# Low weight parts of 24 input-projection blocks by adding transfers, and one buffer set for high and low parts

## The chip, the cores and the metric

The kernel runs on one core of a Trainium2 chip. The metric is the device time of one launch in microseconds (us), a median over runs. Beside it stands one execution recorded by the hardware profiler; its durations are what the text argues from.

## The reference

One layer of a bidirectional hybrid encoder on 512 tokens of 1024 channels, all in float32:

```python
h = rmsnorm(x, mix_norm[l])
p = h @ w_in[l]                                   # 1024 x 9248
rx, ry, qkv, z, ba, gates = jnp.split(p, SPLIT_IDX, axis=-1)
y_rnn = rglru_branch(rx, ry, ...) @ w_rnn_proj[l]
y_dn = deltanet_branch(qkv, z, ba, ...) @ w_dn_proj[l]
g_rnn, g_dn = jnp.split(jax.nn.sigmoid(gates), 2, axis=-1)
x = x + (g_rnn * y_rnn + g_dn * y_dn) @ w_out[l]
h = rmsnorm(x, ffn_norm[l])
gt, up = jnp.split(h @ w_gate_up[l], 2, axis=-1)
x = x + (jax.nn.silu(gt) * up) @ w_down[l]
...
return rmsnorm(x, final_norm)
```

The part that matters here is `p = h @ w_in`: 72 blocks of 128 output columns (and 32 single columns for `ba`).

## The kernel before, in words

**Products in three parts.** A float32 product on TensorE is made of float32r products. A weight block is split into a high part (the weight rounded to float32r) and a low part (the weight less its high part); the activations likewise (`hh`, `hl`). A block's product is high × `hh` + high × `hl` + low × `hh`. `mm3` issues, for a block of 1024 × 128 weights and 512 tokens, 16 matmuls with the high part (`hh` and `hl` in turn, one pair for each of eight slices of 128 rows) and then 8 with the low part: 24 matmuls of 128 × 512. The low part is so wanted 16 matmuls later than the high part.

**How a block's weights come in.** `stage`, through `weights`, plans four steps: SyncE's queue (SP) loads 512 KB into a raw buffer (`wraw`, four of them), ScalarE (ACT) copies it into the high part (`whi`, a CAST from float32 to float32r), VectorE (DVE) subtracts the high part from the raw weights into the low part (`wlo`), and TensorE (PE) uses both. There are two `whi` and two `wlo` buffers of 128 × 1024. The first three blocks use buffers of their own (`weights_k`). The blocks of the other weight matrices use the same three tags.

**The order of the work.** The program isn't written in the order in which it runs. Every operation is recorded (`Rec`), with an estimate of its cost and a planned time `plan.t`; a block's load is planned 40 us ahead of its use, its split 12 (`AHEAD`). `Plan.order` then sets one static sequence for each engine by a list scheduler that starts from the table `TIMES`, a starting time for each of some 200 stages. Everything is emitted from that order, so all instructions carry line 384 in the profile and are told apart by tile names. Each engine works strictly in its sequence; waits between engines are semaphores. A buffer that is used again is waited for: the copy into `whi` waits for the last matmul that reads the block before in that buffer.

**Where the 72 blocks lie.** `in_proj` is called for the blocks of the two recurrent branches, of the queries, keys and values of four head groups (`dn_front`), of `dn_z` and of the two gates (`rnn_gate`, `dn_gate`). It appends to `first_tiles`, which so counts the blocks planned. Between them PE works on the recurrences, the small chunk matrices of the delta rule and the output projection. The feed-forward part (`gate_up`, `down_first`, `down_second`) follows from some 640 us on.

GpSimd (POOL) has little to do: constants and nine small loads in the first 14 us, later 48 small multiplications and 32 selects on the delta rule's matrices.

Of the kernel before, what the change touches and what calls it, by code (L numbers as in the profile page):

```python
# [8 lines left out]
F32R = mybir.dt.float32r  # L9
AF = mybir.ActivationFunctionType  # L10
ALU = mybir.AluOpType
# [3 lines left out]
P = 128  # L15
# [3 lines left out]
KD = D // P  # L19
# [13 lines left out]
RELEASE = 200  # L33
LOOK = 40
TIMES = [
# [14 lines left out]
]  # L50
ENGINES = ("PE", "DVE", "ACT", "POOL", "SP")
N2, N4, NW = 15, 24, 4
AHEAD = 12.0
# [271 lines left out]
class Rec:  # L325
# [5 lines left out]
    def __getattr__(self, op):  # L331
        real = getattr(self.real, op)

        def call(*a, **kw):
            args = list(a) + list(kw.values())
            aps = [x for x in args if hasattr(x, "ap") and hasattr(x, "tensor")]
            out = kw.get("out", a[0] if a else None)
            outs = [out] + ([kw["accum_out"]] if kw.get("accum_out") is not None else [])
            ins = [x for x in aps if not any(x is o for o in outs)]
            big = [x for x in ins if elems(x) > 1 or x.space == PSUM]  # L340
            n = max([elems(out)] + [elems(x) for x in ins])
            psum = any(x.space == PSUM for x in aps)
            ptr = sum(1 for x in ins if elems(x) == 1) if n > 1 else 0
            table, tail = None, 0.0
            e = self.eng
            if op == "dma_start":
                tail = max(out.nbytes() / 360.0, 1)
                cost = 450 if e == "SP" else 1000 if e == "POOL" else 60
            elif e == "PE":
                rhs = a[2] if op == "matmul" else a[1]  # L350
                n = elems(out)
                four_ = rhs.dtype == F32
                cols = elems(a[1]) if op == "matmul" else P
                if op == "transpose":
                    cost = 110
                elif four_:
                    cost = 22 if cols == 32 else 76 if cols == 64 else n * 4 / 2.4 + 10
                else:
                    cost = max(n / 2.4, 107) + 13.3
            elif e == "ACT":  # L360
                cost = (51 if psum else 93) + 0.834 * n + 93 * (ptr if n > 1 else len(ins) - 1) + (93 if len(outs) > 1 else 0)
                if op == "activation":
                    cost = max(cost, 200)
                dims = list(out.ap)
                if op == "copy" and len(dims) > 2 and dims[-1][1] <= 64:
                    cost += 100
                if op == "activation":
                    table = Plan.TABLES.get(a[2])
            elif e == "DVE":
                if op == "reciprocal":  # L370
                    cost = 69 + 6.25 * n
                elif op == "tensor_tensor":
                    cost = 69 + 1.042 * n
                elif op == "tensor_tensor_scan":
                    cost = 69 + 2.08 * n
                elif op == "scalar_tensor_tensor":
                    cost = 130 + 1.042 * n + (70 if len(outs) > 1 else 0)
                elif op == "transpose":
                    cost = 68 + (2.0 if n > 512 else 1.1) * n
                else:  # L380
                    cost = 68 + (1.042 if psum else 0.521) * n + 61 * ptr
            else:
                cost = {"memset": 35 + 0.834 * n, "affine_select": 140 + 0.886 * n}.get(op, 240 + 1.2 * n)
            self.plan.add(e, lambda: real(*a, **kw), outs, ins, cost, tail, table)  # L384

        return call
# [3 lines left out]
def trunk(ctx: ExitStack, tc: tile.TileContext, x, mix_norm, w_in, rg_conv_w, rg_conv_b, rg_wa, rg_ba, rg_wx, rg_bx,  # L390
# [3 lines left out]
    plan = Plan(nc)  # L394
    V, A, G, T = Rec(plan, "DVE", nc.vector), Rec(plan, "ACT", nc.scalar), Rec(plan, "POOL", nc.gpsimd), Rec(plan, "PE", nc.tensor)
    Q = Rec(plan, "SP", nc.sync)
# [3 lines left out]
    wp = ctx.enter_context(tc.tile_pool(name="wp", bufs=2))  # L400
# [14 lines left out]
    def new(pool, shape, tag, bufs, dt=F32):  # L415
        return plan.tile(pool, shape, dt, tag, bufs, nm(tag))
# [13 lines left out]
    def four(dt=F32, shape=(P, 2, 512)):  # L430
        return new(t4, shape, "t4", N4, dt)
# [17 lines left out]
    def f(ap):  # L449
        return ap.bitcast(F32)  # L450
# [143 lines left out]
    first_tiles = []  # L594

    def stage(src, shape, view=lambda t: t, admit=()):

        now = plan.t
        raw = new(wp, shape, "wraw", NW)
        hi = new(wp, shape, "whi", 2, F32R)  # L600
        lo = new(wp, shape, "wlo", 2, F32R)
        plan.t = now - 40
        for dst, s_ in src(raw):
            Q.dma_start(dst, s_)
        plan.t = now - AHEAD
        plan.admit = admit
        A.copy(view(hi), view(raw))
        plan.admit = ()
        V.tensor_tensor(view(lo), view(raw), f(view(hi)), ALU.subtract)
        plan.t = now  # L610
        return hi, lo

    def weights(src, kk, m=P, admit=()):
        return stage(lambda raw: [(raw[:, :kk, :m], src)], (P, 8, P), lambda t: t[:, :kk, :m], admit)

    def parts_of(src, hi, lo, ahead):
        now = plan.t
# [23 lines left out]

    def in_proj(col, po=None, admit=()):
        spend(5.2)
        hi, lo = (weights_k if len(first_tiles) < 3 else weights)(win[:, :, col:col + P], KD, P, admit)
        po = mmb() if po is None else po
        mm3(po, hi, lo, lambda k: hh[:, k, :], lambda k: hl[:, k, :], KD, 2 if len(first_tiles) < 3 else 1)
        first_tiles.append(col)
        return po
# [16 lines left out]
    G.dma_start(dtb, dn_dt_bias[0].rearrange("d h -> (d h)").partition_broadcast(P))  # L665
    G.dma_start(alog, dn_a_log[0].rearrange("d h -> (d h)").partition_broadcast(P))
    braw = new(wp, (P, 8, P), "wraw", NW)
    bhl = new(wp, (P, 8, P), "whi", 2, F32R)
    Q.dma_start(braw[:, :, 0:32], win[:, :, C_BA:C_BA + 32])
    A.copy(bhl[:, :, 0:32], braw[:, :, 0:32])  # L670
    V.tensor_tensor(bhl[:, :, 32:64], braw[:, :, 0:32], f(bhl[:, :, 0:32]), ALU.subtract)
# [618 lines left out]
        T.matmul(po, xl[:, cs_], wh, start=False, stop=stop, skip_group_check=add)  # L1290

    def halves(src, own=False):
        hi, lo = (new(wp, (P, 2, 512), t, 2, F32R) if own else four(F32R) for t in ("whi", "wlo"))
        parts_of(src, hi, lo, 0)
        return [(hi[:, i, :], lo[:, i, :]) for i in range(2)]

# [150 lines left out]
    def gate_up(n):  # L1447
        spend(10.2)
        now = plan.t
# [7 lines left out]
        for t, x_, y_ in ((t1, b11, b12), (t2_, t1, b22), (t3, b12, b22), (t4_, t2_, b21)):  # L1457
            V.tensor_tensor(t, x_, y_, ALU.add)
        plan.t = now
        gh_, gl_ = new(wp, (P, 8, P), "whi", 2, F32R), new(wp, (P, 8, P), "wlo", 2, F32R)  # L1460
        parts_of(rg, gh_, gl_, AHEAD)
        w7 = {"1": (gh_[:, 0:4, :], gl_[:, 0:4, :]), "2": (gh_[:, 4:8, :], gl_[:, 4:8, :])}
        ah, al = new(wp, (P, 8, P), "whi", 2, F32R), new(wp, (P, 8, P), "wlo", 2, F32R)
        bh, bl = four(F32R, (P, 8, P)), four(F32R, (P, 8, P))
        for i, (name, src, hi, lo) in enumerate((("6", t2_, ah, al), ("7", t3, ah, al), ("5", t1, bh, bl), ("4", t4_, bh, bl))):
            j = 4 * (i % 2)
# [68 lines left out]
    def down_first(j):  # L1535
# [1 line left out]
        spend(5.5)  # L1537
        now = plan.t
        r1, r2 = new(wp, (P, 2, 512), "wraw", NW), new(wp, (P, 2, 512), "wraw", NW)
        hi, lo = new(wp, (P, 2, 512), "whi", 2, F32R), new(wp, (P, 2, 512), "wlo", 2, F32R)  # L1540
        t2_ = keep2[j // 8][:, j % 8, :]
        plan.t = now - 40
        Q.dma_start(r2, sums[j])
# [177 lines left out]
```

## Time and profile before

| | |
|---|---|
| median of 3 runs | 1054.76 us (1054.02 to 1055.81) |
| profiled execution | 1052.97 us, of which the span 1051.1 |
| granted TensorE clock | 0.999 |
| busy: PE, DVE, ACT, POOL | 1037.1, 891.1, 689.5, 54.4 us |
| moved | 134.35 MB, mean 128 GB/s |

The profiled execution is one launch; its span runs from the first to the last instruction, and 1.9 us of its time lie around the span. "PEld" is TensorE's weight load, which runs beside its matmuls. In a group's row stand: line, engine, operation, result and operands, shape and count, then busy time in us and the mean of one in ns, then idle time ahead of the group and what ended it. In a row of the timeline stand start and duration in us, and in brackets the idle time ahead of it and its releaser.

### The profile page before, as it was taken

What the parts mean: (1) busy time and instruction counts of PE and PEld (TensorE: products, weight loads), DVE (VectorE), ACT (ScalarE), POOL (GpSimd) and SP (SyncE); (2) the same over time, 40 slices, a digit from 0 to 9 for tenths busy, and PEclk for the clock granted to TensorE, in tenths of its full rate; (3) what the DMA queues carried; (4) which work ended last, traced back from release to release, by engine and by line L of the source; (5) the groups of instructions that cost most, each with busy time, mean ns of one, the idle gap of its engine ahead of it and who ended that gap; (6) DMA issues with size and microseconds to landing.
All of it is one profiled execution on the core that took longest, in us unless ns stands there. A gap on an engine that the chain in (4) does not pass through costs nothing.

```text
span 1051.1 us, 17768 instructions
## 1 busy us (share of the span) xinstructions
PE 1037.1 (99%) x6707; PEld 905.0 (86%) x6707; DVE 891.1 (85%) x1650; ACT 689.5 (66%) x1265; POOL 54.4 (5%) x109
## 2 busy tenths in 40 slices
PE   8999999999999999999999999999999999999997
PEld 7888788888888978888788798889999999998886
DVE  7769989658894898589489748999999999889997
ACT  7799898696638868564765434578554554456564
POOL 2000000202000222010020000000000000000000
PEclk9999999999999999999999999999999999999999
DMA  9422223225342246523213414597456443326632
GB/s 281 121 70 80 81 61 110 71 66 145 101 117 60 74 113 193 182 79 105 57 41 91 141 32 150 188 332 253 139 157 198 147 143 109 122 85 216 215 107 80
DMA packets 177396, 134.35 MB, mean 128 GB/s; under 512 B 6400, under 2 KB 161168, under 8 KB 177312
## 3 DMA queue, kind: packets, MB, share of 16 engines
q1 hardware_dynamic: 175840, 129.95, 40.7%
q10 hardware_dynamic: 1184, 3.15, 0.8%
q8 instruction: 52, 0.85, 0.3%
q14 instruction: 32, 0.26, 0.1%
q0 software_dynamic: 288, 0.13, 0.1%
HBM read 121.12 MB, written 12.09 MB: 127 GB/s over the span
## 4 chain that ended last, share of the span: by engine, by line
PE 91%; DVE 5%; ACT 2%; issue 1%; DMA 1%; ACTq 0%; SPq 0%; DVEq 0%
PE mm L384 53%; PE ax L384 23%; PE st L384 15%; DVE t L384 3%; DVE na L384 1%; ACT t L384 1%; DVE wlo L384 1%; DMA wraw<-in_w_in_dram 1%; ACT hh L384 0%; ACTq L384 0%; ACT L384 0%; ACT whi L384 0%; SPq L384 0%; DVE so L384 0%; DVE hl L384 0%
## 5 line engine op out<-in xcount | busy, mean ns | idle before, releaser
L384 DVE TENSOR_TENSOR t<-t,t 128x512 fp32r<-128x512 f32 (+26 forms) x501 | 249.4, 512 | 24.1 <-ACT t L384 15.8
L384 PE MATMUL mm<-hh,whi 128*128 128x512 f32 (+2 forms) x648 | 228.1, 362 | 0.1
L384 PE MATMUL mm<-hl,whi 128*128 128x512 f32 (+2 forms) x648 | 228.0, 361 | 0.0
L384 ACT CAST whi<-wraw 128x1024 fp32r<-128x1024 f32 (+3 forms) x139 | 130.3, 939 | 122.6 <-PE mm L384 74.9
L384 DVE TENSOR_TENSOR wlo<-wraw,whi 128x1024 fp32r<-128x1024 f32 (+2 forms) x138 | 150.6, 1092 | 40.8 <-ACT whi L384 19.6
L384 PE MATMUL ax<-t,t 128*128 128x512 f32 (+3 forms) x1134 | 156.9, 291 | 1.6 <-issue 1.6
L384 PE MATMUL mm<-hh,wlo 128*128 128x512 f32 (+1 forms) x632 | 147.3, 364 | 0.1
L384 PEld LDWEIGHTS ax<-t,t 128*128 128x128 f32 (+1 forms) x1134 | 123.1, 161 | 21.5 <-issue 3.5
L384 PEld LDWEIGHTS mm<-hh,whi 128*128 128x128 f32 (+1 forms) x648 | 121.6, 188 | 17.5 <-DVE whi L384 0.3
L384 PEld LDWEIGHTS mm<-hl,whi 128*128 128x128 f32 (+1 forms) x648 | 121.6, 188 | 17.1
L384 PEld LDWEIGHTS mm<-hh,wlo 128*128 128x128 f32 x632 | 108.6, 189 | 17.7 <-DVE wlo L384 0.5
L384 ACT CAST t<-t 128x512 fp32r<-128x512 f32 (+2 forms) x148 | 94.9, 654 | 43.7 <-DVE t L384 33.9
L384 DVE SCALAR_TENSOR_TENSOR t<-mm,par,t 128x511 f32<-128x511 f32 (+1 forms) x108 | 80.2, 743 | 18.7 <-ACT t L384 17.7
L384 ACT ACT_TABLE_LOAD x66 | 84.7, 1283 | 6.5 <-DVE so L384 2.0
L384 PE MATMUL mm<-t,whi 128*128 128x512 f32 x320 | 83.2, 397 | 1.2 <-DVE t L384 1.2
L384 PE MATMUL mm<-t,t 128*128 128x256 f32 (+1 forms) x420 | 80.3, 330 | 0.0
L384 PEld LDWEIGHTS mm<-t,whi 128*128 128x128 f32 x320 | 59.0, 188 | 13.1 <-issue 1.6
L384 PEld LDWEIGHTS mm<-t,t 128*128 128x128 f32 x420 | 63.8, 190 | 6.6
L384 ACT ACTIVATE t<-t 128x128 f32<-128x128 f32 (+4 forms) x86 | 47.4, 561 | 31.4 <-DVE t L384 29.9
L384 ACT CAST t<-wraw 128x1024 fp32r<-128x1024 f32 (+1 forms) x55 | 49.2, 896 | 23.3 <-DMA wraw<-in_w_gate_up_dram 14.5
L384 DVE TENSOR_TENSOR t<-wraw,t 128x1024 fp32r<-128x1024 f32 (+1 forms) x55 | 56.6, 1032 | 1.1 <-ACT t L384 0.7
L384 PE MATMUL mm<-t,wlo 128*128 128x512 f32 x160 | 42.9, 394 | 0.0
(208 smaller groups left out, 1685.5 us busy)
## 6 DMA issues: line engine op xcount, KB each, us to landing
wraw<-in_w_in_dram SPq DMA_DIRECT2D x72, 512.0 KB, 3.7
wraw<-in_w_gate_up_dram SPq DMA_DIRECT2D x44, 512.0 KB, 4.4
wraw<-in_w_rnn_proj_dram SPq DMA_DIRECT2D x16, 384.0 KB, 3.5
wraw<-in_w_out_dram SPq DMA_DIRECT2D x12, 512.0 KB, 3.5
t<-in_w_down_dram SPq DMA_DIRECT2D x11, 512.0 KB, 7.1
sums<-t SPq DMA_DIRECT2D x11, 512.0 KB, 5.1
wraw<-sums SPq DMA_DIRECT2D x11, 512.0 KB, 3.4
wraw<-in_w_down_dram SPq DMA_DIRECT2D x22, 256.0 KB, 3.3
```

Source lines behind the costliest of these rows:

```text
L384: self.plan.add(e, lambda: real(*a, **kw), outs, ins, cost, tail, table)
```

## The change

- `weights_d` is new. It loads the raw block as before, lets ACT copy the high part, lets ACT write the negated high part into the low buffer, and then has POOL issue a transfer (`accum_op=ALU.add`) that adds the raw block, 512 KB from one on-chip buffer to another, to what stands in the low buffer: raw − high. DVE has no part in it. ACT's two steps are planned 14 us ahead of use in place of 12.
- `in_proj` uses it from the 49th block planned on, for 24 blocks of 72.
- The tags `whi` and `wlo`, two buffers each, become one tag `wx` with four, for all that used them.
- The planner takes twice the moving time for an adding transfer.
- `TIMES` holds new numbers, so the order of the whole program is another.

```diff
 TIMES = [
-    -176998, -159417, -176656, -106634, -96501, -159195, -96162, -70221, 191167, -94063, -87550, -69365, -34065,
+    -162283, -159297, -163526, -108037, -92752, -158970, -94346, -59098, 168648, -70151, -72611, -51972, -22916,
...
             if op == "dma_start":
-                tail = max(out.nbytes() / 360.0, 1)
+                tail = max(out.nbytes() / 360.0, 1) * (2 if "accum_op" in kw else 1)
...
         raw = new(wp, shape, "wraw", NW)
-        hi = new(wp, shape, "whi", 2, F32R)
-        lo = new(wp, shape, "wlo", 2, F32R)
+        hi = new(wp, shape, "wx", 4, F32R)
+        lo = new(wp, shape, "wx", 4, F32R)
...
+    def weights_d(src, admit):
+
+        now = plan.t
+        raw, hi, lo = new(wp, (P, 8, P), "wraw", NW), new(wp, (P, 8, P), "wx", 4, F32R), new(wp, (P, 8, P), "wx", 4, F32R)
+        plan.t = now - 40
+        Q.dma_start(raw, src)
+        plan.t = now - AHEAD - 2
+        plan.admit = admit
+        A.copy(hi, raw)
+        plan.admit = ()
+        A.activation(lo, f(hi), AF.Copy, scale=-1.0)
+        G.dma_start(lo, raw, accum_op=ALU.add)
+        plan.t = now
+        return hi, lo
...
         spend(5.2)
-        hi, lo = (weights_k if len(first_tiles) < 3 else weights)(win[:, :, col:col + P], KD, P, admit)
+        if len(first_tiles) < 48:
+            hi, lo = (weights_k if len(first_tiles) < 3 else weights)(win[:, :, col:col + P], KD, P, admit)
+        else:
+            hi, lo = weights_d(win[:, :, col:col + P], admit)
...
-    bhl = new(wp, (P, 8, P), "whi", 2, F32R)
+    bhl = new(wp, (P, 8, P), "wx", 4, F32R)
...
-        gh_, gl_ = new(wp, (P, 8, P), "whi", 2, F32R), new(wp, (P, 8, P), "wlo", 2, F32R)
+        gh_, gl_ = new(wp, (P, 8, P), "wx", 4, F32R), new(wp, (P, 8, P), "wx", 4, F32R)
```

(The other buffers of `halves`, `gate_up` and `down_first` change their tags in the same way.)

What the new order does at one place, around a gate block of `dn_gate` or `rnn_gate` (`mm932_1012` is its result). Before, DVE had the subtraction between small vectors of the delta rule (`na`, `dns`, `t` are its working tiles):

```order
L384 TENSOR_TENSOR wlo853_933<-wraw851_931,whi852_932 128x1024
L384 TENSOR_TENSOR t21013_1093<-mm1009_1089,t497_177 128x512
L384 TENSOR_SCALAR n2842_922<-dssq836_916 128x8
L384 RECIPROCAL n2842_922<-n2842_922 128x8
L384 TENSOR_TENSOR dns865_945<-beta68_148,n2842_922 128x16
L384 TENSOR_TENSOR dnse866_946<-dns865_945,ge83_163 128x16
L384 TENSOR_TENSOR wlo931_1011<-wraw929_1009,whi930_1010 128x1024
L384 SCALAR_TENSOR_TENSOR na867_947<-ax870_950,dns865_945,t4868_948 128x2x128
```

Both subtractions are gone from DVE. In the changed order ACT has the copy and the negation, one behind the other:

```order
L384 ACTIVATE wx964_1044<-wx963_1043 128x1024
L384 ACT_TABLE_LOAD
L384 ACTIVATE t495_175<-mm949_1029 128x512
L384 CAST wx930_1010<-wraw929_1009 128x1024
L384 ACTIVATE wx931_1011<-wx930_1010 128x1024
```

The negation `wx931_1011` stands right behind the copy of the same block, between evictions of other blocks' results. POOL's sequence, which had only its multiplications here:

```order
L384 DMA wx948_1028<-wraw946_1026 128x1024
L384 TENSOR_SCALAR t2894_974<-t4808_888,dnse866_946 128x128 x4
L384 TENSOR_SCALAR t2902_982<-t4808_888,dnse866_946 128x128 x4
L384 TENSOR_SCALAR t2911_991<-t4808_888,dnse866_946 128x128 x4
L384 DMA wx849_929<-wraw847_927 128x1024
L384 DMA wx964_1044<-wraw962_1042 128x1024
L384 DMA wx931_1011<-wraw929_1009 128x1024
L384 DMA wx960_1040<-wraw958_1038 128x1024
```

The "DMA" rows are the adding transfers; six stand in a row from `wx849_929` on. On PE, in the changed order, the end of one block (`mm965_1045`) and the start of the next:

```order
L384 MATMUL mm965_1045<-hh19_99,wx963_1043 128x512
L384 MATMUL mm965_1045<-hl20_100,wx963_1043 128x512
L384 MATMUL mm965_1045<-hh19_99,wx964_1044 128x512 x8
L384 MATMUL mm932_1012<-hh19_99,wx930_1010 128x512
L384 MATMUL mm932_1012<-hl20_100,wx930_1010 128x512
```

The last two rows come eight times each, then the 8 matmuls with `wx931_1011`, then the next block in the same way (`wx959_1039` high, `wx960_1040` low). The negation into `wx960_1040` waits for the last of the 8 matmuls with `wx964_1044`, whose buffer it takes; that into `wx931_1011` for the last with `wx849_929`.

More of the change, by code (lines that the diff above doesn't have):

```diff
@@ L1292, in halves @@
     def halves(src, own=False):
-        hi, lo = (new(wp, (P, 2, 512), t, 2, F32R) if own else four(F32R) for t in ("whi", "wlo"))
+        hi, lo = (new(wp, (P, 2, 512), "wx", 4, F32R) if own else four(F32R) for _ in range(2))
         parts_of(src, hi, lo, 0)
@@ L1459, in gate_up @@
         plan.t = now
-        gh_, gl_ = new(wp, (P, 8, P), "whi", 2, F32R), new(wp, (P, 8, P), "wlo", 2, F32R)
+        gh_, gl_ = new(wp, (P, 8, P), "wx", 4, F32R), new(wp, (P, 8, P), "wx", 4, F32R)
         parts_of(rg, gh_, gl_, AHEAD)
         w7 = {"1": (gh_[:, 0:4, :], gl_[:, 0:4, :]), "2": (gh_[:, 4:8, :], gl_[:, 4:8, :])}
-        ah, al = new(wp, (P, 8, P), "whi", 2, F32R), new(wp, (P, 8, P), "wlo", 2, F32R)
+        ah, al = new(wp, (P, 8, P), "wx", 4, F32R), new(wp, (P, 8, P), "wx", 4, F32R)
         bh, bl = four(F32R, (P, 8, P)), four(F32R, (P, 8, P))
@@ L1539, in down_first @@
         r1, r2 = new(wp, (P, 2, 512), "wraw", NW), new(wp, (P, 2, 512), "wraw", NW)
-        hi, lo = new(wp, (P, 2, 512), "whi", 2, F32R), new(wp, (P, 2, 512), "wlo", 2, F32R)
+        hi, lo = new(wp, (P, 2, 512), "wx", 4, F32R), new(wp, (P, 2, 512), "wx", 4, F32R)
         t2_ = keep2[j // 8][:, j % 8, :]
```

26 rows, old and new, of the table TIMES are left out of this document.

## The prediction

> **What bounds the kernel now.** I read the page's busy shares and chain first, then TensorE's waits, then the stretch in which the 24 blocks lie.
>
> ```profile
> PE 1037.1 (99%) x6707; PEld 905.0 (86%) x6707; DVE 891.1 (85%) x1650; ACT 689.5 (66%) x1265; POOL 54.4 (5%) x109
> ...
> PE 91%; DVE 5%; ACT 2%; issue 1%; DMA 1%; ACTq 0%; SPq 0%; DVEq 0%
> ```
>
> TensorE (PE) is busy for 1037.1 of 1051.1 us and is 91% of the chain that ended last. VectorE (DVE), which the change relieves, is 5% of it. A change that removes no matmul can win only what PE waits for, so I list these waits.
>
> ```profile
> engine line waited for: us in total, times, longest us
> PE ax L384 <- DVE ident L384: 2.6, 1, 2.6
> PE ax L384 <- issue: 1.6, 1, 1.6
> PE mm L384 <- DVE hl L384: 1.3, 2, 0.8
> PE mm L384 <- DVE t L384: 1.2, 1, 1.2
> PE ax L384 <- DVE t L384: 0.6, 3, 0.3
> PE st L384 <- ACT hh L384: 0.2, 1, 0.2
> ```
>
> `ident` and `hl` are waits of the first 30 us, where the order of the work hardly changes. What is left: 1.6 + 1.2 + 0.6 + 0.2 = 3.6 us. The three largest stalls in the middle are these rows of the timeline, of PE and of its weight loads (PEld):
>
> ```profile
> 393.44 2.74 PE L384 MATMUL mm<-t,whi 128*128 128x512 f32 x11 [1.20 <-DVE t L384]
> ...
> 470.99 0.39 PE L384 MATMUL mm<-hl,whi 128*128 128x512 f32 x1
> ...
> 471.22 0.39 PE L384 MATMUL mm<-hh,whi 128*128 128x512 f32 x1
> ...
> 471.68 1.70 PEld L384 LDWEIGHTS mm<-hh,wlo 128*128 128x128 f32 x8 [0.50 <-DVE wlo L384]
> ...
> 508.06 0.26 PE L384 MATMUL ax<-t,t 32*32 32x32 f32 x7 [1.57 <-issue]
> ```
>
> The middle one costs PE less than its 0.50: the matmul before it starts at 471.22, so 0.46 lies between two starts that are otherwise 0.23 apart (471.22 behind 470.99): 0.23 lost. The third names no engine, and nothing in the change touches it.
>
> ```profile
> 400.00:500.00 100.00, 99.92 (x727) 84.27 (x726) 79.50 (x202) 62.11 (x139) 11.38 (x20) 1.00 0.47 143
> 500.00:580.00 80.00, 78.43 (x635) 67.16 (x634) 58.38 (x146) 51.52 (x125) 5.30 (x12) 1.00 0.22 60
> 700.00:900.00 200.00, 199.76 (x1620) 196.80 (x1620) 196.08 (x344) 116.60 (x212) 0.00 (x0) 1.00 0.54 169
> ```
>
> The columns are the stretch, its length, then busy time of PE, PEld, DVE, ACT and POOL, granted clock, DMA share, GB/s. Where the changed blocks lie (some 340 to 650 us) DVE is busy 73 to 80%, with PE at 98 to 100%; VectorE is full only from 700 us on, which the change does not relieve.
>
> **The change, part by part.** The durations:
>
> ```profile
> L384 DVE TENSOR_TENSOR wlo<-wraw,whi 128x1024 fp32r<-128x1024 f32 x95 | 116.9, 1230 | 28.2 <-ACT whi L384 11.8 <-PE mm L384 9.8 <-ACT t L384 5.2
> ...
> L384 ACT CAST whi<-wraw 128x1024 fp32r<-128x1024 f32 x95 | 99.9, 1052 | 81.9 <-PE mm L384 50.3 <-PE ax L384 13.9 <-PE st L384 7.1
> ...
> L384 ACT ACTIVATE t<-t 128x1024 f32<-128x1024 f32 x22 | 23.1, 1058 | 0.2
> ```
>
> *Removed from DVE:* 24 subtractions of 1.230 us, 29.5 us. They lie beside PE, so the gain is only in the waits that end on DVE. The stall at 393.4 is such a one; the chain followed back from 420 us holds the subtractions themselves:
>
> ```profile
> by line: PE mm L384 61.1%; DVE t L384 23.0%; DVE wlo L384 7.5%; PE ax L384 5.3%; issue 3.2%
> ```
>
> 7.5% of that window of 40 us (380 to 420) is 3.0 us, more than the stall of 1.2. I count the stalls at 393.4 and 471.7 as won: 1.2 + 0.2 = **−1.4 us**. The bound is nothing on one side, 3.6 + 0.2 = 3.8 us on the other.
>
> *Added to ACT:* 24 negations of 1.058 us, 25.4 us, and five more instructions. ACT is busy 62 to 64% in this stretch and PE waits for it there for 0.2 us in all. I cost it at nothing on its own; the cover is ACT's idle third, and the order below shows where each negation must be in time. Its duration counts in the next item.
>
> *Added to PE's inputs:* a low part is now complete only after a chain: its buffer comes free (the last matmul of an earlier block), ACT negates, POOL issues, the transfer lands. These rows give its first pieces:
>
> ```profile
> 476.39 0.39 PE L384 MATMUL mm<-hl,whi 128*128 128x512 f32 x1
> ...
> 476.82 1.05 ACT L384 CAST whi<-wraw 128x1024 fp32r<-128x1024 f32 x1 [0.44 <-PE mm L384]
> ```
>
> ```profile
> 468.70 0.98 ACT L384 ACTIVATE t<-t,ngc 128x128 f32<-128x128 f32 x3
> ...
> 469.82 0.64 POOL L384 TENSOR_SCALAR_AFFINE_SELECT t<-t 128x512 f32<-128x512 f32 x1 [1.21 <-ACT t L384]
> ```
>
> From the start of the freeing matmul to ACT 476.82 − 476.39 = 0.43; the negation 1.06; from ACT's end to POOL 469.82 − 469.68 = 0.14. With D, the transfer from issue to landing, the chain takes L = 1.63 + D.
>
> How long does the order leave? With four buffers a low part takes one that the second block before it gave free (in the order's rows of PE, `wx_1040` the buffer of `wx_1044`). In between PE has the 8 + 16 high matmuls and low matmuls of another block and the block's own 16: 40 matmuls, by the rate of this row:
>
> ```profile
> 104.69 5.44 PE st L384 x24
> ```
>
> 5.44 / 24 = 0.227 us, so 40 of them are 9.1 us. I counted this for all 24 blocks in the changed order, with the other matmuls in between at their own intervals. Seven blocks have over 13 us, eight 10.9 to 12.9 (four of them 10.9, 11.1, 11.1 and 11.1), two 10.2. The seven shortest have 8.6, 8.7, 8.9, 9.3, 9.7, 9.7 and 10.0 us. PE waits where L is longer.
>
> D has no row: no transfer in the trace adds, and none goes from one on-chip buffer to another. The nearest:
>
> ```profile
> wraw<-in_w_in_dram SPq DMA_DIRECT2D x72, 512.0 KB, 3.7
> ...
> t<-in_x_dram SPq DMA_DIRECT2D x4, 512.0 KB, 5.9
> ...
> gcr<-t SPq DMA_DIRECT2D x1, 32.0 KB, 1.5
> ...
> dtb<-in_dn_dt_bias_dram POOLq DMA_DIRECT2D x1, 8.0 KB, 5.5
> alog<-in_dn_a_log_dram POOLq DMA_DIRECT2D x1, 8.0 KB, 5.5
> ```
>
> ```profile
> 8.24 0.54 POOL L384 DMA_DIRECT2D alog<-in_dn_a_log_dram  x1 [1.40 <-DMA t<-in_rg_conv_w_dram]
> ```
>
> A load of 512 KB takes 3.7: the lower bound. A transfer of POOL's queue takes 5.5 for only 8 KB; 512 KB cost 3.7 − 1.5 = 2.2 more than 32 KB, and the adding transfer has two streams to read: 5.5 + 2 × 2.2 = 9.9, the upper bound. But POOL's transfers ran in the first 14 us (the last of them from 8.24), in which the input's loads of 512 KB took 5.9 in place of 3.7, so part of the 5.5 is crowding. I take 5.0 for the fixed part, near POOL's own rows, and for the data 3.3, one and a half times 2.2 (a second read, one write): **D = 8.3**, L = 9.9. The seven shortest then wait 1.3 + 1.2 + 1.0 + 0.6 + 0.2 + 0.2 + 0 = **+4.5 us**. At D = 7.0 nothing waits (L = 8.6); at 9.9 (L = 11.5) the nine wait 2.9 + 2.8 + 2.6 + 2.2 + 1.8 + 1.8 + 1.5 + 1.3 + 1.3 = 18.2, and the four next 0.6 + 0.4 + 0.4 + 0.4: 20.0.
>
> The Trainium skill's page "DMA: Bandwidth & Descriptors", section "Anatomy of one DMA — SWDGE (gpsimd) path", fits a GpSimd transfer by 2.0 us plus the bytes at 436 GB/s: as an estimate 3.2 us for 512 KB and 4.4 for twice that. By it nothing would wait and the sum would be −1.4; POOL's rows of 5.5 us for 8 KB speak against its 2.0.
>
> *Queues behind the new waits.* On ACT a negation that waits for its buffer holds up what stands next: in the order of the change another block's copy or an eviction, some us ahead of need. On POOL the next transfer waits behind the one ahead, but only for its issue (0.54 us in the row of 8.24); twelve small multiplications stand between two of them. SP's loads wait for raw buffers that an adding transfer now gives free; SP was that early:
>
> ```profile
> SPq L384 <- DVE wlo L384: 510.1, 109, 22.3
> ```
>
> 510 us of waiting for low parts in 109 waits, 4.7 each, means loads are issued long before need: nothing.
>
> *One set of four buffers.* High and low parts now rotate together; the same four buffers of 512 KB, none more. Its effect is in the counted room. *Refit:* the number of matmuls is unchanged, PE's rows go from 4432 to 4428. I price the new order at nothing, with 1.5 us to both sides (about half of the 3.8 above).
>
> **Sum:** −1.4 + 4.5 = +3.1 us on the profiled execution's 1052.97, 1056.1. The three runs have a median of 1054.76, 1.8 above that execution; so 1057.9, said as **1058.0**.
>
> **Rivals.**
>
> (1) *The transfer lands in time, and VectorE's stalls go: faster.* One mechanism: D under 7.0, so L under the shortest room of 8.6 us. For it speaks that POOL's rows come from a crowded start and that DMA is busy only 22 to 47% here; a load of 512 KB with a fast queue has 3.7. Against it stands the 5.5 for 8 KB. Price −1.4 to −3.8: about −2.8, so 1052.0. The point is D = 7.0, from which the first block waits.
>
> (2) *Near the point: no change.* D of 7.0 to 7.9: the stalls (at 7.9, L = 9.5: 0.9 + 0.8 + 0.6 + 0.2 = 2.5) cancel the gain: −1.4 to +1.1, about 1054.8. PE is at 99% and everything else is hidden.
>
> (3) *The transfer takes far longer.* At D = 11, L = 12.6, the nine blocks wait 9 × 1.1 = 9.9 more than at 9.9 and those of 10.9 to 13 come in: over 30 us, about 1085. It would need GpSimd to be kept from its work, or the data to move far slower than any load here; POOL is busy for 11.4 of 100 us at 400 to 500, beside a DVE at 80%, and nothing of the page's chain is POOL's. The Trainium skill's "SBUF — State Buffer", section "SBUF: two separate sides", tells that a VectorE operation in a two-port mode locks GpSimd out of writing descriptors; no run here shows it.
>
> That the change does not do what it says I exclude: the order has the 24 transfers on POOL and 24 subtractions fewer on DVE.
>
> **How the numbers follow.** Forecast (D 7.9 to 9.9) 0.38; (1) 0.28; (2) 0.19; (3) 0.15. A measurement of this kernel tells about 0.2%, 2.1 us, from no change. The forecast gives slower for 0.36 and same for 0.02; (1) faster for 0.22 and same for 0.06; (2) same for 0.16 and faster for 0.03; (3) slower for 0.14 and, if hidden after all, same for 0.01. In all: faster 0.25, same 0.25, slower 0.50. The range reaches from the gain of 3.8 (1054.76 − 3.8 = 1051.0) to most of the forecast's upper end: D = 9.4, L = 11.0, gives 2.4 + 2.3 + 2.1 + 1.7 + 1.3 + 1.3 + 1.0 + 0.8 + 0.8 + 0.1 = 13.8, less 1.4: 1067.2, said as 1068.0. The forecast's own range is 1055 to 1068.
>
> **What would show it.** In the profile of the change: the landing time of `wx` transfers on POOL's queue (8.3 forecast; under 7.0 is rival 1). PE or PEld waiting for "DMA wx" at the low matmuls of the seven blocks (some 4.5 us in all), most of it between 390 and 550 us and one near 647. No wait for DVE at 393 and 472. DVE busy about 862 us, ACT about 715 or more, POOL with 24 more issues. The forecast is wrong if PE waits for no `wx` transfer, or if the refit alone moves more than 1.5 us.

## The result

The changed kernel takes 1052.47 us (median of 9 runs, 1051.53 to 1052.81) against 1054.76 (9 runs, 1053.10 to 1055.81): a ratio of 0.9978, 95% interval 0.9968 to 0.9989. It is faster by 2.3 us. Forecast was slower by 3.2; the time lies inside the range of 1051.0 to 1068.0, on the other side of the time before. On three later occasions the changed kernel had 1052.35, 1052.05 and 1052.18, the kernel before 1054.59, 1054.09 and 1054.78.

The page's head and chain of the changed kernel (its profiled execution: 1052.81 us):

```profile
span 1051.0 us, 17876 instructions
...
PE 1037.1 (99%) x6707; PEld 905.0 (86%) x6707; DVE 869.5 (83%) x1626; ACT 706.7 (67%) x1287; POOL 75.7 (7%) x133
...
PE 86%; DVE 8%; ACT 2%; DMA 2%; issue 1%; SPq 1%; ACTq 0%; DVEq 0%
```

The work went where it was meant to go: 22 us less on DVE, 17 more on ACT, 21 more on POOL. PE is busy to the tenth as before, and the two profiled spans (1051.1 and 1051.0) hardly differ. The gain of the medians is not in these two pages; that is the first thing to explain. The adding transfers, in the list of issues and by tile:

```profile
wx<-wraw POOLq DMA_DIRECT2D x24, 512.0 KB, 5.3
```

```profile
DMA to landing us min/median/max: 4.5/5.3/9.0
```

The median from issue to landing is 5.3 us (forecast: 8.3). PE's waits, to be laid beside those of before:

```profile
PE ax L384 <- DMA gain1r<-in_mix_norm_dram: 2.9, 1, 2.9
PE ax L384 <- DVE t L384: 2.3, 3, 1.2
PE mm L384 <- DVE hl L384: 1.3, 2, 0.8
PE mm L384 <- ACT hh L384: 0.2, 1, 0.2
PE ax L384 <- ACT ax L384: 0.2, 1, 0.2
```

None is for a transfer into `wx`. None is named "issue" either: the wait of 1.6 us at 508.06 is gone. The stalls at 393 and 472 are gone too, but PE's waits for the tiles `t` of DVE are no shorter than before (2.3 us; they were 1.2 + 0.6). They stand at other places, as the timeline shows:

```profile
498.54 0.74 PE L384 MATMUL ax<-t,na 32*32 32x32 f32 x64 [0.68 <-DVE t L384]
```

```profile
897.64 1.70 PE L384 MATMUL ax<-t,t 128*128 128x256 f32 x12 [1.18 <-DVE t L384]
```

The second lies in the feed-forward part, where the change relieves nothing. So these theories were tried: A, the gain is VectorE's relief; B, it is the new order; and, when both had failed, E, it is the stall named "issue" together with what follows it.

### The profile page after: what moved, and what is told of

Read it like the earlier page. It is cut to its first block, busy times and chain, and to the rows that moved or that the text cites. A ratio compares the mean times of both kernels' runs of the same rounds, so it can differ in the third digit from the quotient of the medians.

```text
span 1051.0 us, 17876 instructions
## 1 busy us (share of the span) xinstructions
PE 1037.1 (99%) x6707; PEld 905.0 (86%) x6707; DVE 869.5 (83%) x1626; ACT 706.7 (67%) x1287; POOL 75.7 (7%) x133
## 4 chain that ended last, share of the span: by engine, by line
PE 86%; DVE 8%; ACT 2%; DMA 2%; issue 1%; SPq 1%; ACTq 0%; DVEq 0%
PE mm L384 49%; PE ax L384 23%; PE st L384 15%; DVE t L384 6%; ACT t L384 1%; DVE na L384 1%; DVE wx L384 1%; SPq L384 1%; DMA t<-in_w_down_dram 1%; DMA wraw<-in_w_in_dram 1%; DMA gain2r<-in_ffn_norm_dram 0%; ACT wx L384 0%; ACT ax L384 0%; ACTq L384 0%; ACT na L384 0%
## 5 line engine op out<-in xcount | busy, mean ns | idle before, releaser
L384 PE MATMUL mm<-hh,wx 128*128 128x512 f32 (+2 forms) x1280 | 368.8, 363 | 0.1
L384 DVE TENSOR_TENSOR t<-t,t 128x512 fp32r<-128x512 f32 (+25 forms) x501 | 249.3, 511 | 30.3 <-ACT t L384 20.7
L384 PEld LDWEIGHTS mm<-hh,wx 128*128 128x128 f32 (+1 forms) x1280 | 230.4, 188 | 35.4 <-ACT wx L384 0.7
L384 PE MATMUL mm<-hl,wx 128*128 128x512 f32 (+2 forms) x648 | 228.6, 362 | 0.0
L384 ACT CAST wx<-wraw 128x1024 fp32r<-128x1024 f32 (+3 forms) x139 | 129.9, 937 | 90.6 <-PE mm L384 32.9
L384 DVE TENSOR_TENSOR wx<-wraw,wx 128x1024 fp32r<-128x1024 f32 (+3 forms) x115 | 120.7, 1051 | 35.5 <-PE mm L384 16.8
L384 PEld LDWEIGHTS mm<-hl,wx 128*128 128x128 f32 (+1 forms) x648 | 121.7, 188 | 16.8
L384 PE MATMUL mm<-t,wx 128*128 128x512 f32 x480 | 116.6, 394 | 0.0
L384 PEld LDWEIGHTS mm<-t,wx 128*128 128x128 f32 x480 | 89.0, 188 | 18.4 <-issue 0.2
L384 PE MATMUL st<-hh,wx 128*128 128x512 f32 (+1 forms) x224 | 67.7, 375 | 0.0
```

## The experiments

In the two of the first table, and in the one with the doubled transfer, the finished order was held fixed: an entry of it was carried out by another instruction or by two, so PE and SP do the same in the same order.

**The same order with the other way of making low parts.** In the changed order the transfer's entry subtracts on VectorE, and the negation's entry does nothing:

```diff
+        plan.ops[neg] = (plan.ops[neg][0], lambda: None) + plan.ops[neg][2:]
+        plan.ops[add] = (plan.ops[add][0], lambda: nc.vector.tensor_tensor(lo, raw, f(hi), ALU.subtract)) + plan.ops[add][2:]
```

> The changed order to the last instruction on PE and SP, but each of the 24 low parts is subtracted by DVE again, at the place where POOL issued the transfer; no negations, no transfers. Theory A (the gain is VectorE's 29.5 us of relief): the stalls behind DVE come back, about 1054.8 us, level with the kernel before. Theory B (the gain is the new order): 1052.5 us, level with the changed kernel, since PE hides the 24 subtractions. Each has half: about 1053.6.

And in the order of before the subtraction's entry negates on ACT and adds by a transfer:

```diff
+            def negate_and_add():
+                nc.scalar.activation(lo, f(hi), AF.Copy, scale=-1.0)
+                nc.gpsimd.dma_start(lo, raw, accum_op=ALU.add)
+            plan.ops[-1] = (plan.ops[-1][0], negate_and_add) + plan.ops[-1][2:]
```

> The order of before to the last instruction on PE and SP and its two and two buffers, but the 24 subtractions are taken from DVE, and ACT negates and POOL adds in their place. Theory A (relief): about 1052.5 us, and the PE stalls at 393 and 472 us are gone. Theory B (order): about 1054.8 us, level with the kernel before. If the old order leaves less room for the longer chain, PE waits for DMA at low matmuls and it is slower than before, 1056 us or more.

Beside the changed kernel itself (1052.35 us) and the kernel before (1054.59); the ratios and their intervals come from all the runs and not from the two medians:

| order | low parts of the 24 blocks | us | ratio to before |
|---|---|---|---|
| before | subtracted | 1054.59 | 1 |
| before | added by transfer | 1072.79 | 1.0165 (1.0149 to 1.0181) |
| changed | subtracted | 1066.46 | 1.0101 (1.0086 to 1.0116) |
| changed | added by transfer | 1052.35 | 0.9980 (0.9971 to 0.9989) |

Both theories missed, by much more than the gain in question. Each order fits the way for which it was made; with the other way the order of before loses 18 us and the changed one 14. The profiles show where. PE in the order of before with transfers, and in the changed order with subtractions:

```profile
385.04 2.57 PE L384 MATMUL mm<-hh,wlo 128*128 128x512 f32 x6 [3.71 <-DMA wlo<-wraw]
```

```profile
506.66 1.08 PE L384 MATMUL ax<-t,na 32*32 32x32 f32 x64 [4.18 <-DVE t L384]
```

In the first the chain is longer than the room that the old order leaves: ACT's negation ran at 379.08 behind four copies, the transfer was issued at 380.45 and landed at 384.99. In the second a subtraction of 1.23 us stands on DVE at 502.21, ahead of the transposes (to 506.5) for which PE waits; it is a part of that wait, which was 0.68 in the changed kernel. Another part of both losses is the clock: these two profiles have a mean granted clock of 0.992 and 0.991, against 0.999.

**The planner's own answer.** Two kernels left the ordering to the planner: the change with the old table `TIMES`, and the new table with subtractions (`if len(first_tiles) < 72` in `in_proj`).

> The change with the old table of times: adding transfers and one set of four buffers, the planner orders the work anew around the negations and transfers with its own rules, but its table is that of before. In the fixed order of before the transfers cost 18 us. Theory C (the gain needs an order that was fitted to the longer chain): slower than the kernel before, 1058 to 1070 us. Theory A (VectorE's relief, wherever it is put): 1052 to 1054 us.

> The change with the new table and one set of four buffers, but the planner is given subtractions on DVE for the 24 blocks and orders them by its rules. In the fixed order of the change they cost 14 us. Theory C (each order is fitted to its own durations): slower than the kernel before, 1057 to 1066 us. Theory B (the new table is better by itself): 1052 to 1054 us.

Measured: 1069.18 us (ratio 1.0141, 1.0121 to 1.0160) and 1058.79 (1.0034, 1.0021 to 1.0047), beside 1054.81 for the kernel before. Theory C was right: without its refit the change is a loss of 14 us. Transfers and table can only be judged together.

**The rooms that I had counted.** This one keeps the changed order and doubles the chain's last link:

```diff
+        def twice(add=plan.ops[-1][1]):
+            nc.gpsimd.dma_start(lo, lo)
+            add()
```

> The changed kernel with each of the 24 adding transfers behind a plain transfer of the low buffer onto itself, which leaves its contents alone: D, from issue to landing, goes from 5.3 to some 10 us and the order stays. By the rooms that I counted (8.6 to 10.2 us for nine blocks), a chain of 1.6 + 10 us makes PE wait some 20 us in all: about 1072 us. The rival, that the rooms are larger than counted since PE is held up by other things too: under 1058 us.

The two transfers, and the first row of PE's waits:

```profile
wx<-wx POOLq DMA_DIRECT2D x24, 512.0 KB, 4.0
wx<-wraw POOLq DMA_DIRECT2D x24, 512.0 KB, 4.6
```

```profile
PE mm L384 <- DMA wx<-wraw: 20.3, 12, 2.6
```

From the first issue to the second landing it is 9.5 us in the median. PE waits 20.3 us in 12 waits, where the count of the rooms had said "some 20 us" for 10 us. The time is 1076.08 (ratio 1.0217, 1.0193 to 1.0240), 4 us above the 1072 expected: behind several of these waits the clock is lower for a while (mean granted clock 0.995 in the median run, 0.990 in the profiled one, which was the slowest; 0.999 in the profile of the changed kernel). So far as a sum can show it, the rooms were right; D, the 8.3 us of the prediction, was not.

**Where the medians part: more profiles of before.**

> The kernel before unaltered, for a second profile of it: its runs spread from 1052.5 to 1056.5 us and the profiled one was 1053.0. If the spread comes from PE waits that vary from run to run, a slower profile shows longer or more waits than the first (stalls over 0.2 us in the middle then add to more than 4.5 us); if it lies in the rate of the matmuls, the waits stay and the intervals grow.

The two executions took 1054.88 and 1054.70 us, near the median; the first profile, with 1052.97, was a short one. Counting matmuls in the trace, all three agree to 0.2 us up to the 3000th (506 us) and to 0.4 from the 3250th on; in between, the first took 27.55 us and the others 29.2 and 29.6. The windows behind the stall at 506, for the first profile and then for the second (columns as in the prediction; the granted clock is third from the end):

```profile
507.00:509.00 2.00, 0.94 (x10) 0.81 (x10) 0.00 (x0) 2.00 (x4) 0.00 (x0) 1.00 0.00 0
509.00:511.00 2.00, 2.00 (x10) 1.64 (x10) 0.00 (x0) 1.92 (x7) 0.00 (x0) 1.00 0.04 8
511.00:513.00 2.00, 2.00 (x16) 1.41 (x15) 0.40 (x1) 1.53 (x4) 0.00 (x0) 1.00 0.00 0
```

```profile
507.00:509.00 2.00, 0.94 (x9) 0.81 (x9) 0.00 (x0) 1.99 (x5) 0.00 (x0) 0.83 0.00 0
509.00:511.00 2.00, 2.00 (x7) 1.54 (x6) 0.00 (x0) 1.93 (x6) 0.00 (x0) 0.50 0.03 8
511.00:513.00 2.00, 2.00 (x9) 1.62 (x8) 0.49 (x1) 1.44 (x4) 0.00 (x0) 0.82 0.00 0
```

The stall is 1.57, 1.66 and 1.97 us in the three; but behind it the clock falls to 0.50 for some 3 us in the second and third profile and not in the first. The stretch is 1.7 and 2.0 us longer, and this explains why the one profile lay 1.8 us under the median. The runs without a profile agree: of 21 runs of the kernel before on one occasion, the seven with a mean granted clock of 0.999 took 1053.25 to 1054.29 us, the ten with 0.997 or less 1054.47 to 1056.26. In the changed kernel's profile, without the stall, the clock stays at 1.00 there.

**What the stall is.** PE has just done 89 of 96 small matmuls (32x32) and stops in the middle (here in the second profile of before). The same in the new table with subtractions, after 62 of 96; and the run of 96 in the changed kernel, which PE passes without a stop:

```profile
505.45 0.95 PE L384 MATMUL ax<-t,t 32*32 32x32 f32 x89
508.06 0.26 PE L384 MATMUL ax<-t,t 32*32 32x32 f32 x7 [1.66 <-issue]
```

```profile
512.95 0.74 PE L384 MATMUL ax<-t,t 32*32 32x32 f32 x62
516.06 0.43 PE L384 MATMUL ax<-t,t 32*32 32x32 f32 x34 [2.37 <-issue]
```

```profile
500.56 1.02 PE L384 MATMUL ax<-t,t 32*32 32x32 f32 x96
```

Loads and matmuls counted from the start of PE's program, both stop near the same place, after record 6043 and 6047, though the small matmuls begin at record 5866 in one and 5924 in the other. Counted with what PE's sequencer leaves in the trace, both stop after record 6081, and so do all eight such stalls of the kept traces. It is a place in the instruction stream, not in the work. The trace has a queue for the stream; the page of before lists it:

```profile
q8 instruction: 52, 0.85, 0.3%
```

52 transfers of 16 KB in the launch. One of them starts at 505.80 in the first profile, takes 0.99 us, and PE goes on at 508.06. In each of the eight stalls PE goes on 2.3 to 2.6 us after such a transfer began. 96 small matmuls and their loads start within 0.83 us where nothing stops them, so the reading is that PE runs through its instructions faster than the next 16 KB come. In the changed kernel the run ends at record 6047 of this count, 34 short of the place. The Trainium skill ("Runtime: NRT & Kernel Launch", section "Instruction fetch mechanics") says that each engine's sequencer fetches its program in blocks of 16 KiB, 256 instructions, and that this is mostly hidden. The block size agrees with these transfers; that it is hidden does not hold here, for 1.6 to 2.4 us.

**Moving the place.** If that is so, some 180 more records ahead of the run let the run begin only about the place, behind slower matmuls, and nothing else need change. In the first attempt small matmuls of ones (each leaves two matmuls in the trace) replaced warm-up matmuls of the head:

> The kernel before, with its order on every engine; only three of the ten warm-up matmuls of the head (128x128 of ones into an unused bank) are replaced by 48 of 32x32, 1.4 us of PE time by about the same. That is some 180 records more of loads and matmuls ahead of the run of 96 small matmuls at 505 us. Theory E (the stall of 1.6 us in that run is PE out of instructions: an instruction load of 16 KB begins at 505.8 and PE stops after record 6046 in three kernels): the place moves out of the run, the stall and the slower clock behind it are gone, 3.3 to 3.8 us less than the kernel before, about 1051.2. Rival F (PE waits for a result that the profile doesn't name): the stall stays, 1054.8 us.

> The changed kernel with its order on every engine; one of the ten warm-up matmuls of the head is replaced by 16 of 32x32, some 60 records more. Theory E: record 6046 now falls into the run of 96 small matmuls at 500 us (it ended 30 records ahead of it), PE stops there after about 80 of 96 for some 2 us, named issue, and the clock falls behind it: 1055.5 to 1056.3 us, the gain of the change gone. Rival F: nothing changes, 1052.4 us.

In the profiles the place moved as expected: no "issue" wait in the first, one of 2.39 us in the second. The times decided nothing: 1054.59 and 1051.91 us (ratios 0.9997, 0.9988 to 1.0006, and 0.9983, 0.9973 to 0.9993). The second should have lost the gain of the change (1055.5 or more was expected), and it didn't. The small matmuls take 3.3 us in the head, so the first lost there what it won at 506 (in its profile PE is some 1.7 us late from the head up to 506 and 0.2 early behind it). That profile is of a short run, 1052.48 us; three of its 11 runs are like it, and the other eight took 1054.35 to 1054.97 with a granted clock of 0.998 or 0.999. What those lose, no profile shows, so not every spread of 2 us comes from this stall. A better pair carries the same 44 small matmuls, once ahead of the run, once behind it:

```diff
+            def small_first(real=plan.ops[j][1]):
+                for _ in range(22):
+                    nc.tensor.matmul(po[0:32, 0:32], ones[0:32, 0:32], ones[0:32, 0:32], start=True, stop=True)
+                real()
+            plan.ops[j] = (plan.ops[j][0], small_first) + plan.ops[j][2:]
```

> The kernel before, its order unchanged; ahead of two of its blocks (at some 73 and 105 us) 22 matmuls of 32x32 of ones go into the bank that the block then overwrites: 176 records of loads and matmuls more, in front of the run of 96 small matmuls at 505 us, some 1.2 us of PE time. Theory E (PE is out of instructions after record 6046; the stall costs 1.75 us and in most runs 1.7 us of slower clock behind it): the place moves out of the run, 3.4 less and 1.2 more: about 1052.4 us, and no issue wait at 506 us. Rival F (the wait is for a result): 1055.8 us with the wait.

> The control: the same 44 small matmuls ahead of two products of the feed-forward part, behind the run at 505 us, so its place in the instruction stream stays. Both theories: the wait named issue stays and the small matmuls cost their own time, 1054.5 + 1.2 = about 1055.7 us.

| | us | ratio to before (1054.75) |
|---|---|---|
| 44 small matmuls ahead of the run | 1054.24 | 0.9999 (0.9989 to 1.0008) |
| the same behind it | 1057.59 | 1.0032 (1.0020 to 1.0045) |

The run of 96 in the two timelines:

```profile
508.98 1.02 PE L384 MATMUL ax<-t,t 32*32 32x32 f32 x96
```

```profile
505.68 0.95 PE L384 MATMUL ax<-t,t 32*32 32x32 f32 x89
508.59 0.26 PE L384 MATMUL ax<-t,t 32*32 32x32 f32 x7 [1.95 <-issue]
```

The same instructions, another place: 1057.59 − 1054.24 = 3.35 us, forecast from stall and clock (1.75 + 1.7) as 3.4. In the earlier variant the run of 96 begins two records short of the place, and PE passes it without a stop. The small matmuls themselves cost 2.8 us by the later variant against before (I had said 1.2); in both profiles they stand 32 ns apart on one part of the array, so their cost drops out of the difference. Theory E holds for the kernel before; F, a result that the profile doesn't name, falls.

**Without that cost.** The last variant puts the 44 small matmuls ahead of PE's first instruction, where PE waits anyway, on four parts of the array in turn:

> The kernel before, its order unchanged; the 44 small matmuls now stand ahead of PE's first instruction, where PE has nothing to do until 2.6 us, and work in four parts of the array in turn. Theory E: the place after record 6046 leaves the run of 96 small matmuls as in the early variant (3.35 us less than the late one) and the head hides their cost: 1054.6 - 3.35 = about 1051.3 us, under the changed kernel's 1052.3, with no issue wait at 506. Without that, 1054.6 or more.

Its head and its run of 96:

```profile
1.08 1.39 PE L499 MATMUL ax<-ones 32*32 32x32 f32 x88 [1.08 <-POOL ones L384]
2.62 0.27 PE L384 MATMUL ax<-ident,gain1r 8*128 8x8 f32 x1
```

```profile
506.11 1.02 PE L384 MATMUL ax<-t,t 32*32 32x32 f32 x96
```

1051.89 us (11 runs, 1051.51 to 1052.99), ratio 0.9974 (0.9965 to 0.9983); the changed kernel beside it 1052.18 (11 runs, 1051.20 to 1053.96), 0.9980 (0.9971 to 0.9989). The intervals overlap: the kernel before, without its stall, is level with the changed one. It is the lowest median of the study, not a proven best.

**The reverse, still half open.** A second profile of the changed kernel with the place moved into its run:

> A second profile of the shifted changed kernel, whose runs spread from 1050.2 to 1055.1 us while the one profiled was the slowest, with a wait of 2.6 us named issue. Theory E: the wait is there again, and its length or the clock behind it differs; if the run is fast and shows no such wait, the place in the stream does not decide alone.

1052.72 us, with the wait again (1.97 us) and the clock at 1.00 behind it. In both profiles of this variant the stall behind VectorE at 896 is gone: PE comes later there, and the wait for DVE takes the lost time up. So the stall costs the changed kernel little as long as the clock stays (in the slowest run, 1055.12, whose profile is the first, it fell to 0.50). Why some of its runs are as short as 1050.2 us isn't explained.

**The wait at 896.** One experiment tried to take VectorE's load down there: in eight feed-forward blocks one addition went to POOL.

> The changed kernel with its order; in eight of the twenty feed-forward blocks (the 7th to the 14th) one addition of 128x512 goes from DVE to POOL, 8 x 0.5 = 4 us of DVE in the stretch where it is 97 to 99% busy. Theory G (behind 650 us the changed kernel is held by DVE, whose chain ends in the PE stall of 1.3 to 1.5 us at 896): that stall goes and the time is 1.2 to 1.5 us less, 1050.8 us. Rival: POOL takes longer for the addition or DVE is slowed beside it, 1052.3 us or more.

1054.14 us (0.9997, 0.9988 to 1.0006), some 2 above the changed kernel on its other occasions. The rival held. POOL's row, VectorE's for the same addition in the kernel before, and the wait of PE that came with it:

```profile
L1478 POOL TENSOR_TENSOR t<-wraw 128x512 f32<-128x512 f32 x8 | 15.4, 1923 | 229.7 <-ACT t L384 97.5 <-DMA wraw<-in_w_gate_up_dram 76.6 <-DVE t L384 34.5
```

```profile
L384 DVE TENSOR_TENSOR t<-wraw 128x512 f32<-128x512 f32 x24 | 16.6, 691 | 0.0
```

```profile
784.65 1.69 PE L384 MATMUL mm<-t,t 128*128 128x256 f32 x12 [0.84 <-DVE t L384]
```

The addition takes 1.92 us on POOL, nearly three times VectorE's 0.69 (the 0.5 of the expectation is too low; the profile's mean over many shapes is 0.51), and the sums come late at a new place; the wait behind VectorE at 897 is still there with 1.1 us. VectorE's own additions got slower as well: those named `t<-wraw,wraw` took 0.81 us in place of the changed kernel's 0.68. Theory G is neither shown nor refuted by it.

## Why the prediction was wrong

- **What bounds the kernel.** Right: PE at 99%, and only its waits can be won.
- **VectorE's relief, −1.4 us.** This step failed as well. The two stalls went, as said. But the order that made room for the transfers has waits for VectorE of its own (0.68 at 498, 1.18 at 896), and the sum of them is no smaller. So the profile shows no gain of 1.4 us from them.
- **ACT's negations at nothing.** Right for the order that was fitted to them: 0.4 us of PE's waits name ACT, none of them for a `wx`. In the order of before with transfers, PE waited 3.5 us for ACT's `whi`, a part of the loss of 18 us.
- **D = 8.3 us.** This is the step that failed on the sign, a mis-sized term: 5.3 measured, L = 6.9 in place of 9.9, under the shortest room of 8.6. With it the +4.5 us fell away: PE waits for no `wx` transfer, not even the longest of 9.0, and the prediction's own sum would have been −1.4. Rival 1 came in ("lands in time"). Its point of 7.0 was not tested by itself; at 9.5 us PE waited 20.3 us. POOL's rows of 5.5 us for 8 KB were no fixed part: 512 KB on the same queue took less later in the kernel. That the crowded start made them long is likely and not shown. The upper bound of 9.9 was near the longest single one (9.0). The Trainium skill's formula (page "DMA: Bandwidth & Descriptors", section "Anatomy of one DMA — SWDGE (gpsimd) path") gave 3.2 to 4.4; the measurement lies between it and my value, nearer to the page.
- **"The third names no engine, and nothing in the change touches it."** This step failed too, and it hid where time was to be won. The stall named "issue" is a place in PE's instruction stream, and a new order can move what stands there. In the kernel before it is worth 2.9 us (1054.78 − 1051.89) to 3.35 us, more than the other waits of the middle together (1.2 + 0.6 + 0.2); the changed kernel's run of small matmuls ends 34 records ahead of it.
- **The profile against the median.** I took the 1.8 us between them for spread. They were the slower clock behind that same stall, which the one profiled execution had been spared.
- **The refit at nothing, 1.5 us to both sides.** Too narrow: the same transfers without it cost 14 us. Rival 1 had the transfer right, but its size by luck: it gave −2.8 us by VectorE's stalls, and PE's waits for VectorE didn't shrink.

What is shown: D and the waits that didn't come; the stall's place, its price in the kernel before, and that the kernel before without it is level with the change. Not shown is that the missing stall is the whole of the changed kernel's gain: moved back in, it cost nothing at the median (1051.91 us, beside 1052.05 without). The profiles with an undisturbed clock behind the stall lie near those without the stall: 1052.97 in the kernel before and 1052.72 in the shifted one, against 1052.05 to 1052.88 in the changed kernel's four. So most of the 2.3 us is likely the slower clock behind the stall, which most runs of the kernel before have. Only argued is that the changed order got past the place by chance and not by the planner's rules, which hold nothing on instruction loads.

## What to carry to other kernels

A wait that the profile puts down to no engine is still a wait: look whether it sits in a run of very short instructions, and whether it moves when the number of instructions ahead of it changes; a control that adds the same instructions behind it separates the two. Price a change and its refit as one: a fixed order punished another way of making the low parts by 14 to 18 us, six times and more what the change is worth. And before a change of 0.2% is explained from one profile, take a second profile of the kernel before.

## What the runs showed of the hardware

- An adding transfer of 512 KB from one on-chip buffer to another took 4.5 to 9.0 us from issue to landing, median 5.3, with 0.86 to 0.94 us of POOL's time for its issue; a plain one of the same size on the same queue 4.0.
- PE can run out of instructions, as these traces are best read: 96 matmuls of 32x32 and their loads pass in 0.83 us, and at one place of the stream PE stood for 1.6 to 2.4 us while 16 KB came. All eight stalls in the traces have the same place, and PE goes on 2.3 to 2.6 us after the transfer's start.
- A stall of that length can halve PE's granted clock for some 3 us behind it (twice that once), in some executions of the same program and not in others. Of the eight stalls five did; those of 1.57, 1.97 and 2.37 us did not, while 1.66 and another of 1.97 did. The Trainium skill ("TensorE: Matmul & The Clock Gate", section "Part 1: The HAM clock gate (the "warmup" mystery)") tells of a gate at half speed after an idle window of about 3.4 us; here stalls of about 1.7 us among small matmuls were enough, at times.
